# One Hymba block on one core: router and expert weights laid out for contiguous column chunks, and every group's gather made in full precision

## The chip, the cores and the metric

The kernel runs on one core of one Trainium2 chip. The metric is the device time of one execution in microseconds (us); lower is better. The profiler records one execution: its span runs from the first recorded instruction to the last, and the execution's own time is a little longer. Engines are called PE (matrix engine; PEld is its weight loads), DVE (vector), ACT (scalar), POOL and SP (which only issues transfers here).

## What is computed

One encoder block on 512 tokens of width 1024, in float32: two kinds of attention side by side, an output projection, and then a mixture of 32 experts, of which every token uses two. The change touches the mixture only:

```python
h2 = rms_norm(x, g_ffn)                       # x: 512 x 1024, after attention
pg = softmax(h2 @ wg + bg)                    # top 1 of 4 expert groups
le = h2 @ we + be                             # then top 2 of the 8 experts in it
def expert_block(args):                       # xb: the tokens of one expert
    xb, e = args
    return (silu(xb @ w1[e]) * (xb @ w3[e])) @ w2[e]
x = x + combined                              # each token adds its two experts, times its gates
```

w1 and w3 are 1024 x 512 per expert, w2 is 512 x 1024, so an expert has three matrices of 2 MB.

## The kernel before

Attention, projection and router run until about 288 us. From there on 32 experts are worked off in 13 **groups** (`groups`): ten of two experts and three (groups 2, 7 and 12) of four. An expert's weights come as six tiles of 1 MB through a ring of 17 tiles (`slots`, `ring_tile`). SP issues the loads in order (`load_parts`, L715); a load into a ring place waits until PE has read what the place held.

For each group PE goes through these steps, in program order:

- `hidden` (product at L1224): 16 steps. In a step each expert of the group multiplies its own slice of the array's columns (64 columns for two experts, 32 for four), all at once, and a float32 product leaves two records. `hidden` calls what stands in `during[n]` after step n: that is how other work is put between the steps.
- `finish` (L1196) and `turn_hidden` (L1263): small products and transposes that prepare the next two steps.
- `outputs` (L1280): 8 steps of the same kind, with `after[n]` called between them.

Between the steps of a group's `hidden` stand two foreign jobs, both on the array's full width. **Combine** (L1324, L1325) adds the group before into the sum: four blocks of four records, after steps 4, 6, 8 and 10. The **gather** collects the token rows of the next group: a one-hot matrix (`match`, L919, on DVE) times the block's rows `x2`, the result with the model width on partitions, since `hidden` contracts over that. It exists in two forms:

- `gather` / `gather_part` (L928), used for group 0 alone: 32 float32 products of 128 x 128, two records each, the x2 chunk as the weights and the one-hot matrix as the moving operand. The weights of a product are the columns r, r+4, r+8, ... of a half of x2 (every fourth element), because w1, w3 and the router rows were laid out so.
- `quarter` (L1166), used for groups 1 to 12: x2 is split into a rounded half and a remainder (`prepare`: ACT at L1158, DVE at L1159, 192 each in all, two buffers), and the one-hot matrix is the weights. 16 quarters of two records; two quarters are one **lot** of four records. Then the result is copied (`st`, L1172) and transposed back in two `turn`s of four transposes (L1178).

In a group of the steady kind the eight lots of a gather stand so: two in `outputs` of two groups ahead (after steps 4 and 6), six in the following `hidden`, after steps 0, 2, 4, 6, 8 and 10, the last four of them directly behind a combine block. Group 1's gather and that of the group behind `PAUSE` (group 7, whose `hidden` also contains the branch at L1341 for experts with too many tokens) have all eight lots after steps 8 to 15 of `hidden`. Groups 7 and 12 are gathered in hidden 6 and 11. No lots stand in outputs 6 and 11.

Before group 0 there are 48 records of L928, 24 on each side of the router's count (L909, L910, ranked by DVE at L914); 16 more stand in hidden 0 (`first_gather`).

Of the kernel before, what the change touches and what calls it, by code (L numbers as in the profile page):

```python
# [94 lines left out]
def tile_block(ctx: ExitStack, tc: tile.TileContext, a: dict, out: bass.AP):  # L95
# [553 lines left out]
        wv.add(with_split(i, gen))  # L649


    w1 = a["w1"][0].rearrange("e (h p r) f -> e h p (r f)", h=2, p=P)
    w3 = a["w3"][0].rearrange("e (h p r) f -> e h p (r f)", h=2, p=P)
    w2 = a["w2"].rearrange("e c p q j d -> e c p (q j d)")
    NP = NE // 2

# [107 lines left out]
    iota_s = const.tile([P, SLOTS], F32, name="iota_s")  # L764

    def router_loads():
        nc.sync.dma_start(gfp, a["g_ffn"][0].rearrange("(h p r) -> p h r", h=2, p=P))
        raw_r = pool_at.tile([P, KC, 64], F32, tag="qn", name="raw_r", bufs=2)
        parts = {"w_router_g": raw_r[:, 0:1, 0:32], "w_router_e": raw_r[:, 1:5]}
        for n, r in (("w_router_g", 4), ("w_router_e", 32)):  # L770
            parts[n] = parts[n].rearrange("p a b -> p (a b)").rearrange("p (h c) -> p h c", h=2)
            nc.sync.dma_start(parts[n], a[n][0].rearrange("(h p r) c -> p h (r c)", h=2, p=P))
        for src, c0, n in ((a["b_router_g"], 0, 4), (a["b_router_e"], 4, 32)):
            nc.sync.dma_start(rbias[:, c0:c0 + n], bass.AP(tensor=src.tensor, offset=src.offset, ap=[[0, P], [1, n]]))
        nc.gpsimd.iota(desc, pattern=[[-1, 4]], base=4, channel_multiplier=0, allow_small_or_imprecise_dtypes=True)
        nc.gpsimd.iota(iota_s, pattern=[[1, SLOTS]], base=1, channel_multiplier=0,
                       allow_small_or_imprecise_dtypes=True)
        nc.gpsimd.iota(iota_e, pattern=[[1, NE]], base=0, channel_multiplier=0, allow_small_or_imprecise_dtypes=True)
        nc.gpsimd.affine_select(before, ones_f, pattern=[[1, P]], compare_op=ALU.is_gt, fill=0.0,
                                base=0, channel_multiplier=-1)  # L780
        nc.gpsimd.memset(ones_b, 1.0)
        nc.gpsimd.iota(favour, pattern=[[-1, NE]], base=NE - 1, channel_multiplier=0,
                       allow_small_or_imprecise_dtypes=True)
        nc.gpsimd.iota(favour[:, 0:FIXED], pattern=[[-1, FIXED]], base=FIXED, channel_multiplier=0,
                       allow_small_or_imprecise_dtypes=True)
        nc.gpsimd.tensor_scalar(favour[:, 0:FIXED], favour[:, 0:FIXED], 1e6, None, op0=ALU.mult)
        nc.gpsimd.iota(ids, pattern=[[0, 1]], base=0, channel_multiplier=1, allow_small_or_imprecise_dtypes=True)
# [14 lines left out]
    def half_turn(t, h, tag="tr"):  # L802

        xh = x_tile[0][:, t, h * 512:(h + 1) * 512]
        pb = bank(tag)
        xp = xh.rearrange("p (b r) -> p r b", r=4)
        for r in range(4):
            nc.tensor.transpose(pb[:, r * P:(r + 1) * P], xp[:, r], ident)
        x2T[2 * t + h] = pool_raw.tile([P, 4, P], F32, tag="w_raw", name="x2T", bufs=4)
        nc.scalar.copy(x2T[2 * t + h], pb.rearrange("p (k t) -> p k t", k=4))  # L810

# [110 lines left out]
    def gather_part(px, oh, h, ts_):  # L922

        for t in ts_:
            x2 = x_tile[0][:, t, h * 512:(h + 1) * 512].rearrange("p (b r) -> p r b", r=4)
            one = oh[:, t].rearrange("p e s -> p (e s)").bitcast(F32)
            for r in range(4):
                nc.tensor.matmul(px[h][:, r], lhsT=x2[:, r], rhs=one, start=(t == NT - 1 and r == 0),  # L928
                                 stop=(t == 0 and r == 3), skip_group_check=True)
# [206 lines left out]
    def dispatch(oh, p, px=None):  # L1136
# [12 lines left out]
                d["px"] = [bank("sc" if spare else "tr", (P, 4, P)) for _ in range(2)]  # L1149
            gather_part(d["px"], oh, h, ts_)  # L1150

        def prepare(n):

            h, t, q = n // 8, NT - 1 - n // 2 % NT, n % 2
            part = d[n] = wk("part", [P, 2, 256], F32R, bufs=2)
            whole = x_tile[0][:, t, h * 512:(h + 1) * 512].rearrange("p (b r) -> p r b", r=4)[:, 2 * q:2 * q + 2]
            hi, lo = (part[:, m].rearrange("p (r b) -> p r b", r=2) for m in range(2))
            nc.scalar.copy(hi, whole)  # L1158
            nc.vector.tensor_tensor(lo, whole, hi.bitcast(F32), op=ALU.subtract)  # L1159

        def quarter(n, tag="sc"):
            h, t, q = n // 8, NT - 1 - n // 2 % NT, n % 2
            if n % 8 == 0:
                d["rows"] = bank(tag)
            for m in (1, 0):
                nc.tensor.matmul(d["rows"][:, q * 256:q * 256 + 256], lhsT=ohs[t], rhs=d[n][:, m],  # L1166
                                 start=(n % 8 == 0 and m == 1), stop=(n % 8 == 7 and m == 0), skip_group_check=True)
            if n + 2 < 16:
                prepare(n + 2)
            if n % 8 == 7:  # L1170
                d["st"] = wk("st", [P, 512])
                nc.scalar.copy(d["st"], d["rows"])  # L1172

        def turn():
            d["px"] = d["px"] or []
            px = bank("tr", (P, 4, P))
            for r in range(4):
                nc.tensor.transpose(px[:, r], d["st"][:, r * P:(r + 1) * P], ident)  # L1178
            d["px"].append(px)

        def take(h):
            if h == 0:
                xt = None if spare else wk("xt", [P, 2, 4, P])
# [31 lines left out]
            d["oht"], d["gsl"], d["rsl"] = oht, gsl, rsl  # L1215
            yield

        for f in (gather, prepare, quarter, turn, take, finish):
            d[f.__name__] = f
        return d  # L1220

# [62 lines left out]

        return w.rearrange("p (q j d) -> p j q d", j=4, d=256)

    def outputs(t, ht, d, between):

        between, py = iter(between), []
        y = None if isinstance(t["w2", 1, 1], list) else new_y()  # L1290
        for c in range(2):
            py.append(bank("sc"))
            for j in range(4):
                for e, part in enumerate(d["parts"]):
                    w = t["w2", c, e]
                    if isinstance(w, list):
                        for q, wq in enumerate(w):
                            output_product(py[c][:, 256 * q:256 * q + 256], ht, j, part, quarters(wq)[:, j, 0],
                                           q == 0, q == 1)
                    else:  # L1300
                        output_product(py[c].rearrange("p (q d) -> p q d", q=2), ht, j, part, quarters(w)[:, j])
                for f in next(between, ()):
                    f()
            if y:
                put_y(y[0][:, c], y[1][:, c], py[c], d["gsl"])
        return y or put_both(py, d["gsl"])
# [86 lines left out]
    PAUSE = 7  # L1393

    def begin(i):
        d = following[i] = group_dispatch(i)
        d["prepare"](0), d["prepare"](1)

    def call(i, name, *args):
        following[i][name](*args)  # L1400
# [1 line left out]
    for i in range(NG):  # L1402
# [3 lines left out]
        if not last:  # L1406
            rest = ahead if i == 0 else load_parts(i + 1)
            for nxt in islice(rest, 1) if i == PAUSE else rest:
                pass
        during, after = [[] for _ in range(16)], [[] for _ in range(8)]  # L1410
        if i == 0:
            def first_gather(d=d):
                d["gather"](1, (1, 0))
# [3 lines left out]
            during[3] = [turn_places]  # L1417
            during[4] = [first_gather]
            during[7] = [sort_places, partial(begin, 1)]
            during[11] = [lambda d=d: run(d["finish"]("tr"))]  # L1420
        else:
            for n in range(8):
                at_ = (3 if n < 4 else 7) if last else 3 + n // 2 if i == PAUSE else 4 + n // 2 * 2
# [1 line left out]
        if not last:  # L1425
            if i == PAUSE:
                during[7] += [overflow, lambda: list(rest), partial(begin, i + 1)]
                work_on = [(8 + n // 2, "quarter", n) for n in range(16)] + [(13, "turn")]
            elif i + 1 in following and i:
                work_on = [(n // 2 * 2 - 4, "quarter", n) for n in range(4, 16)] + [(6, "turn")]  # L1430
            elif i:
                begin(i + 1)
                work_on = [(n * 12 // 16 + 2, "quarter", n) for n in range(16)] + [(10, "turn")]
            else:
                work_on = [(8 + n // 2, "quarter", n) for n in range(16)] + [(13, "turn")]
            for n, *what in work_on:
                during[n].append(partial(call, i + 1, *what))
        sl = hidden(i, tiles, d, during)
        if not last:
            call(i + 1, "turn")  # L1440
        ht = turn_hidden(sl, iter(()) if last else following[i + 1]["finish"]("o"))
        if last:
            break
        nd = following[i + 1]
        nd["take"](0), nd["take"](1)
        if i + 2 < NG and i + 1 != PAUSE:
            after[0].append(partial(begin, i + 2))
            for n in range(4):
                after[4 + n // 2 * 2].append(partial(call, i + 2, "quarter", n, "mm"))
# [87 lines left out]
```

## Time and profile before

| what | value |
|---|---|
| median of 3 runs | 767.83 us (766.74 to 768.61) |
| the profiled execution's own time | 766.24 us |
| its span | 764.4 us |
| PE busy in the span | 733.8 us (96%) |
| weight loads (PEld) busy | 457.7 us (60%) |
| DVE, ACT, POOL busy | 440.3, 360.0, 91.8 us |
| transfers, mean over the span | 299 GB/s, 228.84 MB |

A mean over the span hides that attention and the experts have different limits, so the experts' stage is read by stretches. In the timeline a row is a run of like instructions: start, length, engine, line, operands, count, and in square brackets an idle time before it with what ended it. Records of PE overlap, so a cost on PE is read from start to start and not by adding up lengths.

### The profile page before, as it was taken

To read this page: it belongs to the slowest core of one execution; us is meant where nothing else is said; L and a number is where in the kernel's file an instruction comes from. 1 tells how busy PE (TensorE), PEld (TensorE's weight loads), DVE (VectorE), ACT (ScalarE), POOL (GpSimd) and SP (SyncE) were. 2 spreads that over 40 slices of the span, in tenths; PEclk is the share of its full clock that TensorE was granted. 3 is DMA by queue.
4 is the path that set the end of the run, shared out by engine and by line. 5 is a ranking of instruction groups with operands and counts; after the bars stand their busy time and mean duration, and the time that the engine had idled before them with its cause. 6 is when DMAs were issued, how large, how long until landed. Compare 5 with 4: busy or idle time off the path is not lost. (4 is left out here: it accounts for less than half of the span.)

```text
span 764.4 us, 13043 instructions
## 1 busy us (share of the span) xinstructions
PE 733.8 (96%) x4748; PEld 457.7 (60%) x4748; DVE 440.3 (58%) x932; ACT 360.0 (47%) x725; POOL 91.8 (12%) x175
## 2 busy tenths in 40 slices
PE   9999999999999999899999999999789999999976
PEld 8899988977889895454444444443234444444223
DVE  4677778776765452565655656563455565565303
ACT  6575867877654421643543434341254344353000
POOL 0302100566663110000000000000000000000000
PEclk9999999999999999999999999999899999999999
DMA  8533111313664955557999999999999999999996
GB/s 312 161 113 91 56 56 55 126 42 111 197 254 172 409 232 208 198 216 316 419 421 420 422 421 419 422 421 419 418 421 421 421 420 420 423 421 420 416 409 258
DMA packets 45902, 228.84 MB, mean 299 GB/s; under 512 B 6885, under 2 KB 9189, under 8 KB 22921
## 3 DMA queue, kind: packets, MB, share of 16 engines
q1 hardware_dynamic: 45688, 227.96, 75.1%
q8 instruction: 38, 0.62, 0.3%
q14 instruction: 32, 0.25, 0.1%
q10 hardware_dynamic: 144, 0.00, 0.0%
HBM read 225.83 MB, written 2.11 MB: 298 GB/s over the span
## 5 line engine op out<-in xcount | busy, mean ns | idle before, releaser
L1158 ACT CAST part<-xs 128x256 fp32r<-128x256 f32 x192 | 119.9, 674 | 121.7 <-PE ps_mm L1166 43.0
L1159 DVE TENSOR_TENSOR part<-xs,part 128x256 fp32r<-128x256 f32 x192 | 115.9, 635 | 58.2 <-ACT part L1158 54.7
L1326 DVE TENSOR_TENSOR sums<-ps_o,sums 128x512 f32<-128x512 f32 x88 | 56.7, 686 | 45.7 <-PE ps_o L1325 45.7
L313 PE MATMUL ps_mm<-w_h,hTl 128*128 128x256 f32 x240 | 69.5, 290 | 0.2
L1224 PE MATMUL ps_mm<-qs,xt 128*64 128x512 f32 (+1 forms) x136 | 68.4, 615 | 1.1 <-DMA qs<-in_w 1.1
L313 PE MATMUL ps_mm<-w_h,hTh 128*128 128x256 f32 x240 | 67.3, 281 | 0.0
L313 PE MATMUL ps_mm<-w_l,hTh 128*128 128x256 f32 x240 | 67.3, 280 | 0.0
L1224 PE MATMUL ps_mm<-mb,xt 128*64 128x512 f32 (+1 forms) x120 | 59.8, 616 | 4.4 <-PEq L1341 4.4
L1224 PE MATMUL ps_mm<-kl,xt 128*64 128x512 f32 (+1 forms) x120 | 60.3, 616 | 0.0
L1224 PE MATMUL ps_mm<-kh,xt 128*64 128x512 f32 (+1 forms) x104 | 50.8, 601 | 0.2 <-DMA kh<-in_w 0.2
L1224 PE MATMUL ps_mm<-w_l,xt 128*64 128x512 f32 (+1 forms) x128 | 50.7, 602 | 0.0
L1224 PE MATMUL ps_mm<-w_h,xt 128*64 128x512 f32 (+1 forms) x120 | 46.8, 601 | 0.0
L313 PEld LDWEIGHTS ps_mm<-w_h,hTl 128*128 128x128 f32 x240 | 45.2, 189 | 1.1 <-DVE hTl L239 0.8
L180 DVE TENSOR_TENSOR w_l<-w_raw,w_h 128x512 fp32r<-128x512 f32 x64 | 44.4, 708 | 1.6 <-ACT w_h L177 1.4
L313 PEld LDWEIGHTS ps_mm<-w_l,hTh 128*128 128x128 f32 x240 | 45.3, 189 | 0.1
L313 PEld LDWEIGHTS ps_mm<-w_h,hTh 128*128 128x128 f32 x240 | 45.2, 188 | 0.0
L518 DVE TENSOR_TENSOR_SCAN p<-p,ones_f 128x513 f32<-128x513 f32 (+3 forms) x32 | 27.5, 859 | 30.6 <-POOL p L513 30.5
L1324 PE MATMUL ps_o<-yl,oht 128*128 128x512 f32 x96 | 43.2, 450 | 0.6 <-DVE sums L1326 0.6
L1253 DVE SCALAR_TENSOR_TENSOR sl<-ps_mm,rsl,sl 128x256 f32<-128x256 f32 x26 | 11.4, 479 | 54.9 <-PE ps_mm L1224 54.9
L1324 PEld LDWEIGHTS ps_o<-yl,oht 128*128 128x128 f32 x96 | 17.9, 187 | 41.8 <-DVE part L1159 24.4
L1267 ACT COPY sl<-ps_mm 128x256 f32<-128x256 f32 x26 | 10.0, 386 | 68.7 <-PE ps_mm L1263 68.7
L177 ACT CAST w_h<-w_raw 128x512 fp32r<-128x512 f32 x64 | 38.2, 621 | 5.2 <-DMA w_raw<-in_w_in 4.9
(299 smaller groups left out, 1781.2 us busy)
## 6 DMA issues: line engine op xcount, KB each, us to landing
qs<-in_w SPq DMA_DIRECT2D x22, 1024.0 KB, 19.8
e<-in_w SPq DMA_DIRECT2D x22, 1024.0 KB, 19.8
kl<-in_w SPq DMA_DIRECT2D x21, 1024.0 KB, 19.8
kh<-in_w SPq DMA_DIRECT2D x21, 1024.0 KB, 19.8
n<-in_w SPq DMA_DIRECT2D x20, 1024.0 KB, 19.8
mb<-in_w SPq DMA_DIRECT2D x20, 1024.0 KB, 19.8
w_h<-in_w SPq DMA_DIRECT2D x20, 1024.0 KB, 19.8
w_l<-in_w SPq DMA_DIRECT2D x20, 1024.0 KB, 19.8
```

What stands on the lines that cost most here:

```text
L177: nc.scalar.copy(part(wh, n), raw[i, n])
L180: eng.tensor_tensor(part(wl, n), raw[i, n], part(wh, n).bitcast(F32), op=ALU.subtract)
L313: nc.tensor.matmul(pb[:, u], lhsT=x(t0 + u, k), rhs=y[:, k], start=first, stop=last, skip_group_check=True)
L518: nc.vector.tensor_tensor_scan(rev, rev, ones_f[:, 0:1].to_broadcast([P, n + 1]), 1.0, op0=ALU.mult, op1=ALU.mult)
L1158: nc.scalar.copy(hi, whole)
L1159: nc.vector.tensor_tensor(lo, whole, hi.bitcast(F32), op=ALU.subtract)
L1224: nc.tensor.matmul(ph[n][part], lhsT=d["xt"][h][:, r, part], rhs=w, start=(h == 0 and r == 0), stop=(h == 1 and r == 3))
L1253: nc.vector.scalar_tensor_tensor(s, ph["w3"][:, c], d["rsl"], s, op0=ALU.mult, op1=ALU.mult)
L1267: nc.scalar.copy(s, pb)
L1324: nc.tensor.matmul(pc, lhsT=oht[:, t], rhs=yl[:, c], start=True, stop=False)
L1326: nc.vector.tensor_tensor(sums[0][:, t, cs], pc, (xs if first else sums[0])[:, t, cs], op=ALU.add)
```

## The change

- On the host, w1, w3, w_router_g, w_router_e and g_ffn get another order of rows, so that a product of `x2` takes 128 neighbouring columns instead of every fourth. The bytes of a load and its rows stay as they were.
- `gather_part` and the transposes for the router (`half_turn`) read neighbouring columns.
- `prepare`, `quarter`, `turn` and the copy `st` are gone. Every group uses `gather`: 32 float32 products in eight lots of four products, that is eight records, after steps 2, 3, 5, 6, 8, 9, 11 and 12 of the `hidden` before (after steps 8 to 15 for group 1 and for the one behind PAUSE). `outputs` has nothing between its steps any more.
- The one-hot matrix of the next group (`begin`) is made at the start of `hidden` instead of in the `outputs` before it. Group 0's `finish` uses another bank of the accumulator memory, "o" for "tr".

The diff, cut to its core:

```diff
-    w1 = a["w1"][0].rearrange("e (h p r) f -> e h p (r f)", h=2, p=P)
-    w3 = a["w3"][0].rearrange("e (h p r) f -> e h p (r f)", h=2, p=P)
+    w1, w3 = (a[n].rearrange("e h p r f -> e h p (r f)") for n in ("w1", "w3"))
...
-        xp = xh.rearrange("p (b r) -> p r b", r=4)
         for r in range(4):
-            nc.tensor.transpose(pb[:, r * P:(r + 1) * P], xp[:, r], ident)
+            nc.tensor.transpose(pb[:, r * P:(r + 1) * P], xh[:, r * P:(r + 1) * P], ident)
...
-            x2 = x_tile[0][:, t, h * 512:(h + 1) * 512].rearrange("p (b r) -> p r b", r=4)
+            x2 = x_tile[0][:, t, h * 512:(h + 1) * 512].rearrange("p (r b) -> p r b", r=4)
             one = oh[:, t].rearrange("p e s -> p (e s)").bitcast(F32)
             for r in range(4):
                 nc.tensor.matmul(px[h][:, r], lhsT=x2[:, r], rhs=one, start=(t == NT - 1 and r == 0),
...
-        def prepare(n):
...
-            nc.scalar.copy(hi, whole)
-            nc.vector.tensor_tensor(lo, whole, hi.bitcast(F32), op=ALU.subtract)
-
-        def quarter(n, tag="sc"):
...
-        def turn():
...
     def begin(i):
-        d = following[i] = group_dispatch(i)
-        d["prepare"](0), d["prepare"](1)
+        following[i] = group_dispatch(i)
...
-            during[11] = [lambda d=d: run(d["finish"]("tr"))]
+            during[11] = [lambda d=d: run(d["finish"]("o"))]
...
-                work_on = [(8 + n // 2, "quarter", n) for n in range(16)] + [(13, "turn")]
-            elif i + 1 in following and i:
-                work_on = [(n // 2 * 2 - 4, "quarter", n) for n in range(4, 16)] + [(6, "turn")]
             elif i:
                 begin(i + 1)
...
+            for n in range(8):
+                at_ = 2 + n * 3 // 2 if i and i != PAUSE else 8 + n
+                during[at_].append(partial(call, i + 1, "gather", n // 4, (NT - 1 - n % 4,)))
         sl = hidden(i, tiles, d, during)
-        if not last:
-            call(i + 1, "turn")
...
-        if i + 2 < NG and i + 1 != PAUSE:
-            after[0].append(partial(begin, i + 2))
-            for n in range(4):
-                after[4 + n // 2 * 2].append(partial(call, i + 2, "quarter", n, "mm"))
-        prev = outputs(tiles, ht, d, after), d["oht"]
+        prev = outputs(tiles, ht, d), d["oht"]
...
+    for n in ("w1", "w3"):
+        data[n] = np.ascontiguousarray(data[n][0].reshape(NE, 2, 4, P, HID).transpose(0, 1, 3, 2, 4))
```

In the lists below x4 counts products, each row is one line of the program on one engine, and the names n, mb, w_h, w_l are ring tiles with weights. PE in `hidden` of group 9, around the first combine block, before:

```order
L1224 MATMUL ps_mm<-n_6557,xt 64x512
L1224 MATMUL ps_mm<-mb,xt 64x512
L1166 MATMUL ps_mm<-part,oh 128x256 x4
L1224 MATMUL ps_mm<-n_6557,xt 64x512
L1224 MATMUL ps_mm<-mb,xt 64x512
L1224 MATMUL ps_mm<-w_h,xt 64x512
L1224 MATMUL ps_mm<-w_l,xt 64x512
L1324 MATMUL ps_o<-yl,oht 128x512
L1325 MATMUL ps_o<-yh,oht 128x512
L1324 MATMUL ps_o<-yl,oht 128x512
L1325 MATMUL ps_o<-yh,oht 128x512
L1166 MATMUL ps_sc<-part,oh 128x256 x4
```

The same place in the changed kernel (L1193 is the product of `hidden`, L1291 and L1292 are combine, L926 is the gather):

```order
L1193 MATMUL ps_mm<-n_6032,xt 64x512
L1193 MATMUL ps_mm<-mb,xt 64x512
L926 MATMUL ps_tr<-oh,xs 128x128 x4
L1193 MATMUL ps_mm<-w_h,xt 64x512
L1193 MATMUL ps_mm<-w_l,xt 64x512
L1291 MATMUL ps_o<-yl,oht 128x512
L1292 MATMUL ps_o<-yh,oht 128x512
L1291 MATMUL ps_o<-yl,oht 128x512
L1292 MATMUL ps_o<-yh,oht 128x512
L1193 MATMUL ps_mm<-w_h,xt 64x512
L1193 MATMUL ps_mm<-w_l,xt 64x512
L926 MATMUL ps_tr<-oh,xs 128x128 x4
```

The lot that stood behind the combine block now stands alone one step later, between two steps of `hidden`.

PE in the second half of `outputs` of group 8, before:

```order
L1280 MATMUL ps_sc<-n_6299,sl_6662 64x512
L1166 MATMUL ps_mm<-part,oh 128x256 x4
L1280 MATMUL ps_sc<-kh,sl_6662 64x512
L1280 MATMUL ps_sc<-n_6299,sl_6662 64x512
L1280 MATMUL ps_sc<-kh,sl_6663 64x512
L1280 MATMUL ps_sc<-n_6299,sl_6663 64x512
L1166 MATMUL ps_mm<-part,oh 128x256 x4
```

and in the changed kernel (L1249 is the product of `outputs`):

```order
L1249 MATMUL ps_sc<-n_5865,sl_6109 64x512
L1249 MATMUL ps_sc<-kh,sl_6109 64x512
L1249 MATMUL ps_sc<-n_5865,sl_6109 64x512
L1249 MATMUL ps_sc<-kh,sl_6110 64x512
L1249 MATMUL ps_sc<-n_5865,sl_6110 64x512
```

Both lots have left `outputs`. DVE from `outputs` of group 8 to the first combine of hidden 9, before (xt: the gathered rows, yl: a rounding remainder of the outputs):

```order
L1186 TENSOR_TENSOR xt<-ps_tr,gfp 128x256 x4
L919 TENSOR_TENSOR oh<-rank_s,iota_s 128x512
L1159 TENSOR_TENSOR part<-xs,part 128x256 x2
L1274 SCALAR_TENSOR_TENSOR yl<-ps_sc,gsl,yh 128x512
L1159 TENSOR_TENSOR part<-xs,part 128x256 x4
L1274 SCALAR_TENSOR_TENSOR yl<-ps_sc,gsl,yh 128x512
L1159 TENSOR_TENSOR part<-xs,part 128x256 x4
L1326 TENSOR_TENSOR sums<-ps_o,sums 128x512 x2
```

and in the changed kernel:

```order
L1183 TENSOR_REDUCE rsl<-g_6592 128x1
L1155 TENSOR_TENSOR xt<-ps_tr,gfp 128x256 x4
L1243 SCALAR_TENSOR_TENSOR yl<-ps_sc,gsl,yh 128x512 x2
L917 TENSOR_TENSOR oh<-rank_s,iota_s 128x512
L1293 TENSOR_TENSOR sums<-ps_o,sums 128x512 x8
```

The one-hot match has moved from ahead of both yl to behind both, and the halves are gone.

## Rows read from the trace of the kernel before

**Rows 1.** Stretches: start:end, length, busy PE PEld DVE ACT POOL, PEclk, DMA share, GB/s.

```profile
333.00:366.00 33.00, 32.99 (x164) 14.97 (x164) 20.47 (x42) 14.78 (x28) 0.00 (x0) 1.00 0.67 267
366.00:530.00 164.00, 163.99 (x892) 73.81 (x888) 96.70 (x186) 68.67 (x125) 0.00 (x0) 1.00 1.01 421
...
710.00:758.00 48.00, 40.43 (x308) 15.61 (x300) 11.20 (x20) 3.92 (x9) 0.00 (x0) 1.00 0.96 383
```

**Rows 2.** Waits of the load queue (SPq), whole span: us in all, times, longest.

```profile
SPq L715 <- PE ps_mm L1224: 64.0, 16, 11.9
```

**Rows 3.** Last group: timeline of PE, and a last line from the chain.

```profile
722.30 0.62 PE L1224 MATMUL ps_mm<-kh,xt 128*32 128x512 f32 x1
...
735.14 1.43 PE L1224 MATMUL ps_mm<-n,xt 128*32 128x512 f32 x3
...
738.71 0.40 PE L1280 MATMUL ps_sc<-mb,sl 128*32 128x256 f32 x1
...
754.99 1.91 PE ps_sc L1280 x26
```

**Rows 4.** Timeline before group 0: router transposes and gather on PE, rank on DVE.

```profile
270.58 1.23 PE L808 MATMUL ps_tr<-ident,xs 128*128 128x128 f32 x8
...
275.35 5.84 PE L928 MATMUL ps_tr<-oh,xs 128*128 128x128 f32 x24 [0.29 <-DVE oh L919]
...
281.49 0.23 DVE L914 SCALAR_TENSOR_TENSOR rank<-ps_o,act 128x64 f32<-128x64 f32 x1 [3.38 <-PE ps_o L1050]
```

**Rows 5.** Timeline, PE in attention: float32 products of 128 x 128, neighbouring columns.

```profile
80.69 0.61 PE L607 MATMUL ps_o<-v,pT 128*128 128x128 f32 x4
...
104.50 1.05 PE L607 MATMUL ps_o<-v,pT 128*128 128x128 f32 x8
```

**Rows 6.** Timeline, PE in hidden 0: first_gather between two steps.

```profile
293.59 4.00 PE L928 MATMUL ps_tr<-oh,xs 128*128 128x128 f32 x16
297.52 0.64 PE L1224 MATMUL ps_mm<-kl,xt 128*64 128x512 f32 x1
```

**Rows 7.** Timeline, PE in hidden 9: a lot alone, a combine with a lot.

```profile
611.94 0.59 PE L1224 MATMUL ps_mm<-n,xt 128*64 128x512 f32 x1
...
612.37 0.59 PE L1224 MATMUL ps_mm<-n,xt 128*64 128x512 f32 x1
...
612.90 0.74 PE L1166 MATMUL ps_mm<-part,oh 128*128 128x256 f32 x4
613.57 0.64 PE L1224 MATMUL ps_mm<-n,xt 128*64 128x512 f32 x1
...
617.44 0.59 PE L1224 MATMUL ps_mm<-w_h,xt 128*64 128x512 f32 x1
...
619.58 0.64 PE L1224 MATMUL ps_mm<-w_h,xt 128*64 128x512 f32 x1
```

**Rows 8.** Timeline, PE in hidden 7: a combine block alone between two steps.

```profile
532.77 0.59 PE L1224 MATMUL ps_mm<-kh,xt 128*32 128x512 f32 x1
...
534.44 0.62 PE L1224 MATMUL ps_mm<-w_h,xt 128*32 128x512 f32 x1
```

**Rows 9.** Waits of PE in 288 to 333 us: us in all, times, longest.

```profile
PE ps_sc L1166 <- DVE part L1159: 3.2, 4, 1.6
PE ps_tr L1178 <- ACT st L1172: 0.7, 1, 0.7
```

**Rows 10.** Timeline, PE in group 7: a lot in hidden, a step of outputs.

```profile
555.12 1.01 PE L1166 MATMUL ps_sc<-part,oh 128*128 128x256 f32 x4
...
570.11 0.59 PE L1280 MATMUL ps_sc<-mb,sl 128*32 128x512 f32 x1
...
573.65 1.04 PE L1280 MATMUL ps_sc<-w_h,sl 128*32 128x512 f32 x2 [1.42 <-DMA w_h<-in_w]
```

**Rows 11.** Timeline, DVE around the start of hidden 9.

```profile
605.87 0.68 DVE L919 TENSOR_TENSOR oh<-rank_s,iota_s 128x512 fp32r<-128x512 f32 x1
...
612.90 0.75 DVE L1274 SCALAR_TENSOR_TENSOR yl<-ps_sc,gsl,yh 128x512 fp32r<-128x512 f32 x1
```

More of the change, by code (lines that the diff above doesn't have):

```diff
@@ L766, in router_loads @@
     def router_loads():
-        nc.sync.dma_start(gfp, a["g_ffn"][0].rearrange("(h p r) -> p h r", h=2, p=P))
+        nc.sync.dma_start(gfp, a["g_ffn"])
         raw_r = pool_at.tile([P, KC, 64], F32, tag="qn", name="raw_r", bufs=2)
@@ L771, in router_loads @@
             parts[n] = parts[n].rearrange("p a b -> p (a b)").rearrange("p (h c) -> p h c", h=2)
-            nc.sync.dma_start(parts[n], a[n][0].rearrange("(h p r) c -> p h (r c)", h=2, p=P))
+            nc.sync.dma_start(parts[n], a[n].rearrange("p h r c -> p h (r c)"))
         for src, c0, n in ((a["b_router_g"], 0, 4), (a["b_router_e"], 4, 32)):
@@ L1150, in gather @@
             gather_part(d["px"], oh, h, ts_)
-        def prepare(n):
[L1154 to L1157, printed above, removed]
-            nc.scalar.copy(hi, whole)
-            nc.vector.tensor_tensor(lo, whole, hi.bitcast(F32), op=ALU.subtract)
-        def quarter(n, tag="sc"):
[L1162 to L1172, printed above, removed]
-        def turn():
[L1175 to L1179, printed above, removed]
         def take(h):
@@ L1216, in finish @@
             yield
-        for f in (gather, prepare, quarter, turn, take, finish):
+        for f in (gather, take, finish):
             d[f.__name__] = f
@@ L1285, in quarters, with outputs @@
         return w.rearrange("p (q j d) -> p j q d", j=4, d=256)
-    def outputs(t, ht, d, between):
-        between, py = iter(between), []
+    def outputs(t, ht, d):
+        py = []
         y = None if isinstance(t["w2", 1, 1], list) else new_y()
@@ L1301, in outputs @@
                         output_product(py[c].rearrange("p (q d) -> p q d", q=2), ht, j, part, quarters(w)[:, j])
-                for f in next(between, ()):
-                    f()
             if y:
@@ L1409, in tile_block @@
                 pass
-        during, after = [[] for _ in range(16)], [[] for _ in range(8)]
+        during = [[] for _ in range(16)]
         if i == 0:
@@ L1427, in tile_block @@
                 during[7] += [overflow, lambda: list(rest), partial(begin, i + 1)]
-                work_on = [(8 + n // 2, "quarter", n) for n in range(16)] + [(13, "turn")]
-            elif i + 1 in following and i:
-                work_on = [(n // 2 * 2 - 4, "quarter", n) for n in range(4, 16)] + [(6, "turn")]
             elif i:
                 begin(i + 1)
[L1433 to L1437, printed above, removed]
+            for n in range(8):
+                at_ = 2 + n * 3 // 2 if i and i != PAUSE else 8 + n
+                during[at_].append(partial(call, i + 1, "gather", n // 4, (NT - 1 - n % 4,)))
         sl = hidden(i, tiles, d, during)
-        if not last:
-            call(i + 1, "turn")
         ht = turn_hidden(sl, iter(()) if last else following[i + 1]["finish"]("o"))
@@ L1526 @@
     data["w_o"] = np.ascontiguousarray(data["w_o"][0].reshape(KC // 2, 2, P, 4, 256).transpose(3, 0, 2, 1, 4))
+    for n in ("w1", "w3"):
+        data[n] = np.ascontiguousarray(data[n][0].reshape(NE, 2, 4, P, HID).transpose(0, 1, 3, 2, 4))
+    for n in ("w_router_g", "w_router_e"):
+        data[n] = np.ascontiguousarray(data[n][0].reshape(2, 4, P, -1).transpose(2, 0, 1, 3))
+    data["g_ffn"] = np.ascontiguousarray(data["g_ffn"][0].reshape(2, 4, P).transpose(2, 0, 1))
     data["w2"] = np.ascontiguousarray(data["w2"][0].reshape(NE, 4, P, 2, 2, 256).transpose(0, 3, 2, 4, 1, 5))
```

## Prediction

> **What bounds the kernel now.** I read the stretches first, then the waits, then the timeline around the places that change. Up to about 366 us the transfers don't run full: 267 GB/s at 67% in 333 to 366 us [rows 1], because SP waits for PE to give ring places back (64.0 us in 16 waits, [rows 2]). From 366 to 530 us both are full: PE is busy for 163.99 of 164 us and the transfers move 421 GB/s [rows 1]. PE never waits there, so every microsecond that is added to PE's row between the steps delays the next group. Only in the last group do the transfers win: in 710 to 758 us PE is busy for 40.43 of 48 us [rows 1]. How much PE waits there is read from starts. A record of `hidden` follows the last after 0.43 us (611.94 to 612.37, [rows 7]), a step is two records, 0.86. In hidden 12 the last record begins 16 records after 722.30 less one, so at 728.75 without waits; it begins at 735.14 + 1.43 - 0.59 = 735.98 [rows 3]. That is 7.2 us. Outputs 12 run from 738.71 to 754.99 + 1.91 = 756.90, 18.2 us [rows 3]; the work in them is 32 half-wide records of 0.215 and two sums as large as a combine block (1.26 below), 9.4 us. That is 8.8 us of waiting. So the last group hides up to 16.0 us of added PE time, and the question is whether the change adds more than this, net of what it saves.
>
> **The price of a lot.** An old lot alone: 612.37 to 613.57 is 1.20, less the 0.43 that a record takes anyway, plus 0.05 since the record behind it is longer (0.64 for 0.59): 0.82 [rows 7]. Combine with a lot is 617.44 to 619.58, likewise 1.76 [rows 7]; combine alone is 532.77 to 534.44, 1.26 to 1.29 [rows 8]. So a lot directly behind a combine costs 0.48, and standing alone 0.35 more: that is the price of going from the experts' column slices to the full array and back. The gather's lot of 16 records in hidden 0 goes from 293.59 to 297.52, 3.93; with the 0.53 ahead of a lot (612.37 to 612.90, [rows 7]), less 0.43 and plus 0.05 as above, it cost 4.08 [rows 6]. From 24 records in 5.84 and 16 in 4.00 a record with every fourth column is 0.23 [rows 4, 6], so again 0.35 to 0.4 is left over.
>
> How fast a record with neighbouring columns goes isn't seen in the gather. The nearest row is attention's product of the same shape and type: 4 records in 0.61, 8 in 1.05, 0.11 a record [rows 5]. The ends are 0.11 and 0.23; I take 0.11, since form, type and column order are those of the new gather. A new lot is 8 x 0.11 + 0.35 = **1.24** alone and 8 x 0.11 + 0.03 = 0.91 behind a combine.
>
> A rule speaks about the 0.35. The rows show it on every lot that stands alone. The Trainium skill, "TensorEngine Tiling (Array Packing)", section Key Properties, says that changing the tiling mode, not just the tile, drains the engine. The trace agrees with 0.35 each time. A steady group goes from 8 such excursions to 10 (four combines and six lots alone, against four and four), so without the drain the sum below would be some 7 us lower, an estimate from 2 x 0.35 in 10 groups.
>
> **The sum, in time order.**
> - Before group 0: 48 records go from 0.23 to 0.11, 5.8 us. DVE idled 3.38 us ahead of the rank [rows 4], so it can take the first half's 2.9 us; I take -5.6. The router's transposes take 8 in 1.23 [rows 4] where 8 products with neighbouring columns take 1.05 [rows 5]; 16 stand there with nothing beside them, -0.4. Together **-6.0**.
> - Hidden 0: `first_gather`, 16 x 0.12 = -1.95. The waits for halves and st go, -3.9 [rows 9], two turns go, -0.5 (four records of 0.11 each; the second lies where PE waits for the end of `hidden` anyway, so I count 0.1 for it). The eight lots are taken like those in hidden 7, which span 1.01 for 0.74 [rows 7, 10] and so cost 1.09, not 0.82: 8 x 0.15 = +1.2. Together **-5.1**.
> - Outputs 0 lose two lots, **-1.6**. Group 1's hidden begins 12.7 us earlier.
> - A steady group: six lots at 1.24 and two at 0.91 come, 9.26; four lots at 0.82, four at 0.48 and the turns' 0.5 go, 5.7. **+3.5** each. Eight groups (1 to 5 and 8 to 10): +28.0. Groups 6 and 11 had only six lots, since their outputs held none: +5.1 each, +10.2.
> - Group 7: eight lots at 1.24 for 1.09, without turns and the wait for st: 0. Its outputs lose two lots, -1.6, and a step whose four experts started 3.5 us apart (570.11 and 573.65, waiting for a weight tile, [rows 10]) has its tile in time, since PE comes later: -3.5. Together **-5.1**.
> - The last group then begins -12.7 + 28.0 + 10.2 - 5.1 = 20.4 us later, and its 16.0 us of waits go. For this the last tile must come before it is needed: seven of its 24 tiles wait for places that its own first steps free; at some 20 us for eight tiles in the queue (8 x 1.05 MB at 421 GB/s, [rows 1]) they land about 754 to 757 us, and the last quarter of the outputs then begins near 760. It fits, barely.
>
> 20.4 - 16.0 = **+4.4 us**. The profiled execution took 766.24 us, 1.6 less than the median of the runs; so 770.6 for it and **772.2** against the median of 767.83.
>
> Costed at nothing: ACT's and DVE's halves (192 each) go, since from 366 us on they lie beside PE's full row [rows 1]. Loads keep their bytes. Where the halves' waits go in hidden 0, nothing is late behind them but PE itself.
>
> **Rivals.** (a) **The transfers stay the bound.** Hidden 1 gets all eight lots, +5.1, and so ends 12.7 - 5.1 = 7.6 us earlier; the ring places that it frees come earlier by this, the full transfers begin and end 7.6 us earlier: 767.8 - 7.6 = 760.2. It decides where PE's sum falls below this, 12 us less over the 80 steady lots, 0.15 a lot: a lot at 1.09 or less. For it: PE's records overlap and are partly modelled, and the weight loads are busy for only 73.81 of 164 us [rows 1]. Against it: the price comes from starts, not from lengths. Between them a lot at 1.18 gives no change (4.4 / 80 = 0.06 less). The Trainium skill, "Perfetto Trace Analysis", section Identifying the Most-Contended Engine, warns that matmul busy share doesn't tell how near PE is to its limit, and to go by weight loads. By that rule PE has room at 45% and this rival would be the likely one; the waits of 0 in 366 to 530 us speak against.
> (b) **The new gather isn't faster than the strided one.** A lot is then 8 x 0.23 + 0.35 = 2.2, about 1 us more, 96 lots: some 85 to 90 us, 860. Against it stand attention's rows [rows 5].
> (c) **A new wait for the one-hot matrix.** DVE ends the second yl at 612.90 + 0.75 = 613.65, 1.71 after hidden 9 began, and the match of 0.68 follows [rows 11], so it is done at 2.4; PE reaches the first lot after three steps, 2.6 [rows 7]. 0.2 us of room. If yl is late by 0.5, PE stands 0.3 to 0.4 in each of 11 groups: 3 to 5 us on top, 775 to 777. Behind the waiting PE stand `hidden` itself and the release of its weights.
>
> **How the numbers follow.** The forecast, lots of 1.20 to 1.3 and PE the bound through the stage, has 0.55; rival (c) 0.10 and (b) 0.03. No change within 0.2% (1.5 us, what a measurement of this kernel can tell) needs lots between 1.16 and 1.20: 0.12. Faster has lots below 1.16 and, at its end, (a): 0.20. So slower 0.68, same 0.12, faster 0.20. The range reaches (a) at 760.2 and (c) with lots of 1.28 (+3 us), 781; it leaves out (b) and the tails. The forecast's own range is 769.4 to 777.
>
> **What would show it.** Eight records of the gather in 1.0 to 1.1 us; a steady group taking 3.5 us longer from hidden to hidden; hidden 0 beginning near 282 us; PE without waits in the last group and the transfers below 421 GB/s before it. It is wrong if a lot alone costs under 1.16, if the last group still waits for weights by several us (then the transfers bind), or if PE waits for the match after step 2.

## The result and the profile after

The changed kernel takes **775.09 us** in the median of 4 runs (773.81 to 776.03) against 767.29 us for the kernel before, a ratio of 1.0099 with a 95% interval of [1.0075, 1.0122]: **about 1% slower**. The forecast was 772.2 us, slower. The profiled execution took 774.29 us with a span of 772.6; before it was 766.24 and 764.4.

Stretches of the changed kernel (columns as in [rows 1]):

```profile
366.00:530.00 164.00, 162.55 (x900) 78.57 (x900) 44.95 (x94) 14.51 (x34) 0.00 (x0) 1.00 1.00 413
...
585.00:732.00 147.00, 145.63 (x740) 69.66 (x740) 41.41 (x90) 13.39 (x33) 0.00 (x0) 1.00 0.95 386
732.00:767.00 35.00, 32.98 (x314) 15.41 (x306) 11.97 (x21) 4.11 (x9) 0.00 (x0) 1.00 0.92 355
```

ACT's busy time in 366 to 530 us fell from 68.67 to 14.51 us and DVE's from 96.70 to 44.95 [rows 1]. None of that shows in the time. PE is as full as it was, and the transfers, which moved 419 GB/s in 585 to 732 us of the kernel before, drop to 386: they now have to wait for PE. The waits of the load queue say it directly (288 to 770 us; us in all, times, longest), against 64.0 us in [rows 2]:

```profile
SPq L714 <- PE ps_mm L1193: 219.6, 45, 14.3
```

What a lot costs, in hidden 9 of the changed kernel, alone and behind a combine block, and the start of hidden 10 (timeline, as [rows 7]):

```profile
621.29 0.59 PE L1193 MATMUL ps_mm<-n,xt 128*64 128x512 f32 x1
...
623.44 0.59 PE L1193 MATMUL ps_mm<-n,xt 128*64 128x512 f32 x1
...
623.97 1.16 PE L926 MATMUL ps_tr<-oh,xs 128*128 128x128 f32 x8
625.06 0.64 PE L1193 MATMUL ps_mm<-n,xt 128*64 128x512 f32 x1
...
627.63 0.59 PE L1193 MATMUL ps_mm<-w_h,xt 128*64 128x512 f32 x1
...
629.29 0.64 PE L1193 MATMUL ps_mm<-w_h,xt 128*64 128x512 f32 x1
...
631.87 0.59 PE L1193 MATMUL ps_mm<-w_h,xt 128*64 128x512 f32 x1
...
633.43 1.05 PE L926 MATMUL ps_tr<-oh,xs 128*128 128x128 f32 x8
634.42 0.64 PE L1193 MATMUL ps_mm<-w_h,xt 128*64 128x512 f32 x1
...
658.09 0.59 PE L1193 MATMUL ps_mm<-e,xt 128*64 128x512 f32 x1
```

Alone: 623.44 to 625.06 is 1.62, less 0.43 and plus 0.05 as in the prediction, **1.24 us**. Combine with a lot: 631.87 to 634.42, likewise 2.17; combine alone, 627.63 to 629.29, takes 1.28 here too, so a lot behind it costs 0.89. From hidden 9 to hidden 10 pass 36.80 us. In the kernel before hidden 9 begins at 611.94 [rows 7] and hidden 10 here, 33.07 later:

```profile
645.01 0.59 PE L1224 MATMUL ps_mm<-e,xt 128*64 128x512 f32 x1
```

The part that saves is at the front. Start of hidden 0 in the kernel before, then start of hidden 0 and `first_gather` in the changed one (`first_gather` before: [rows 6]):

```profile
287.66 0.64 PE L1224 MATMUL ps_mm<-bt,xt 128*64 128x512 f32 x1 [0.52 <-DVE xt L1186]
```

```profile
280.66 0.64 PE L1193 MATMUL ps_mm<-bt,xt 128*64 128x512 f32 x1 [0.52 <-DVE xt L1155]
...
286.06 0.59 PE L1193 MATMUL ps_mm<-kl,xt 128*64 128x512 f32 x1
...
286.59 2.05 PE L926 MATMUL ps_tr<-oh,xs 128*128 128x128 f32 x16
...
288.57 0.64 PE L1193 MATMUL ps_mm<-kl,xt 128*64 128x512 f32 x1
```

Sixteen records that spanned 4.00 us [rows 6] span 2.05. The end, from the chain (start, length, what):

```profile
752.87 10.29 DMA qs<-in_w
...
763.20 1.91 PE ps_sc L1249 x26
```

The last tile lands at 763.16 and PE starts its last row 0.04 later, so at the very end PE still waits for weights a little.

### The profile page after: what moved, and what is told of

It reads as the page before. It is cut to its first block, busy times and chain, and to the rows that moved or that the text cites. A ratio compares the mean times of both kernels' runs of the same rounds, so it can differ in the third digit from the quotient of the medians.

```text
span 772.6 us, 13076 instructions
## 1 busy us (share of the span) xinstructions
PE 750.4 (97%) x5036; PEld 476.9 (62%) x5036; DVE 325.8 (42%) x740; ACT 228.9 (30%) x509; POOL 92.2 (12%) x175
## 5 line engine op out<-in xcount | busy, mean ns | idle before, releaser
L926 PEld LDWEIGHTS ps_tr<-oh,xs 128*128 128x128 f32 x768 | 95.0, 192 | 60.7 <-issue 49.7
L926 PE MATMUL ps_tr<-oh,xs 128*128 128x128 f32 x768 | 108.7, 286 | 1.0 <-DVE oh L917 1.0
L1193 PE MATMUL ps_mm<-qs,xt 128*64 128x512 f32 (+1 forms) x136 | 68.7, 616 | 0.0
L1193 PE MATMUL ps_mm<-mb,xt 128*64 128x512 f32 (+1 forms) x120 | 61.1, 619 | 4.3 <-PEq L1308 4.3
L1193 PE MATMUL ps_mm<-kl,xt 128*64 128x512 f32 (+1 forms) x120 | 60.8, 618 | 0.0
L1217 ACT ACTIVATE sl<-ps_mm,rsl 128x256 f32<-128x256 f32 x26 | 10.9, 471 | 159.2 <-PE ps_mm L1193 143.8
L1193 PE MATMUL ps_mm<-w_l,xt 128*64 128x512 f32 (+1 forms) x128 | 52.7, 606 | 0.0
L1193 PE MATMUL ps_mm<-kh,xt 128*64 128x512 f32 (+1 forms) x104 | 52.0, 607 | 0.0
L1193 PE MATMUL ps_mm<-w_h,xt 128*64 128x512 f32 (+1 forms) x120 | 48.5, 606 | 0.0
L1243 DVE SCALAR_TENSOR_TENSOR yl<-ps_sc,gsl,yh 128x512 fp32r<-128x512 f32 (+1 forms) x28 | 19.9, 712 | 64.3 <-ACT yh L1242 61.7
L1291 PE MATMUL ps_o<-yl,oht 128*128 128x512 f32 x96 | 43.1, 449 | 0.6 <-DVE sums L1293 0.6
L1291 PEld LDWEIGHTS ps_o<-yl,oht 128*128 128x128 f32 x96 | 17.9, 187 | 41.8 <-issue 35.1
## 6 DMA issues: line engine op xcount, KB each, us to landing
mb<-in_w SPq DMA_DIRECT2D x20, 1024.0 KB, 13.2
w_l<-in_w SPq DMA_DIRECT2D x20, 1024.0 KB, 13.3
```

Source lines behind the costliest of these rows:

```text
L1193: nc.tensor.matmul(ph[n][part], lhsT=d["xt"][h][:, r, part], rhs=w, start=(h == 0 and r == 0), stop=(h == 1 and r == 3))
L1217: nc.scalar.activation(s, ph["w1"][:, c], AF.Silu, scale=d["rsl"])
L1243: nc.vector.scalar_tensor_tensor(yl, py, gsl, yh.bitcast(F32), op0=ALU.mult, op1=ALU.subtract)
L1291: nc.tensor.matmul(pc, lhsT=oht[:, t], rhs=yl[:, c], start=True, stop=False)
```

## The experiments

All nine were built from the changed kernel or the kernel before. "Changed" below is 775.09 us; times are medians, ratios are to the kernel before on the same chip.

**What makes a lot dear: its records or its standing alone?** First the lots in pairs behind the combine blocks:

```diff
-                at_ = 2 + n * 3 // 2 if i and i != PAUSE else 8 + n
+                at_ = (4 if i and i != PAUSE else 8) + n // 2 * 2
```

> The changed kernel with its eight lots put in pairs: two lots (16 records) directly behind each of the four combine blocks, and in pairs after steps 8, 10, 12 and 14 for group 1 and the group behind PAUSE. Same products, six fewer separate excursions from the experts' column slices per steady group. Theory (an excursion costs 0.35 us, a record 0.11): a pair behind a combine costs 16 x 0.11 = 1.8, a steady group takes 36.8 - 6 x 0.35 = 34.7 us, the last group begins some 23 us earlier than in the changed kernel (near 708), and then the transfers bind again; they run full earlier than before by the 8 to 12 us that group 1 ends earlier, so about 757 us (754 to 760). Rival 1 (records set the price, wherever they stand): 775. Rival 2 (the transfers can't use the earlier start, they bind where they did before): 766 to 768.

756.66 us (755.14 to 757.54), ratio 0.9872 [0.9842, 0.9901]. The same products in other places are 18 us faster. The timeline of PE in hidden 9:

```profile
610.28 0.59 PE L1193 MATMUL ps_mm<-w_h,xt 128*64 128x512 f32 x1
...
611.84 1.95 PE L926 MATMUL ps_tr<-oh,xs 128*128 128x128 f32 x16
613.72 0.64 PE L1193 MATMUL ps_mm<-w_h,xt 128*64 128x512 f32 x1
```

Combine and pair take 3.44 - 0.43 + 0.05 = 3.06; without combine's 1.28 that is 1.78 for 16 records, 0.11 each and nothing on top. A steady group takes 34.72 us, 2.08 less than changed, as six excursions at 0.35 would have it. Rival 1 is out, and so is rival 2: the end did move, to 10 us below the kernel before on the same chip (766.74).

The opposite, every lot cut in two:

```diff
-                at_ = 2 + n * 3 // 2 if i and i != PAUSE else 8 + n
-                during[at_].append(partial(call, i + 1, "gather", n // 4, (NT - 1 - n % 4,)))
+                for m in range(2):
+                    at_ = min(2 + 2 * n + m, 14) if i and i != PAUSE else 8 + n
+                    during[at_].append(partial(call, i + 1, "gather", n // 4, (NT - 1 - n % 4,), (2 * m, 2 * m + 1)))
```

> The changed kernel with every lot cut in two: 16 half lots of four records after steps 2 to 14 of a steady hidden (four of them together after step 14, four behind a combine). Same products; nine excursions stand alone instead of six. Theory (0.35 an excursion): 1.05 us more in each of ten groups, less up to 2 us that the last group still waits for weights: 783 to 786. Rival (records set the price): 775.

784.49 us (783.61 to 785.17), ratio 1.0234 [1.0207, 1.0261], inside the expected band. A half lot alone:

```profile
629.39 0.59 PE L1193 MATMUL ps_mm<-n,xt 128*64 128x512 f32 x1
...
629.92 0.71 PE L926 MATMUL ps_tr<-oh,xs 128*128 128x128 f32 x4
630.56 0.64 PE L1193 MATMUL ps_mm<-n,xt 128*64 128x512 f32 x1
```

1.17 - 0.43 + 0.05 = 0.79. So alone 4 records cost 0.79, 8 cost 1.24 and `first_gather`'s 16 cost 2.51 - 0.43 + 0.05 = 2.13: 0.35 and 0.11 a record, over a factor of four. That an excursion has a price of its own, which does not grow from 4 to 16 records, is shown. That the price is a drain between tiling modes, as the Trainium skill has it ("TensorEngine Tiling (Array Packing)", Key Properties), fits all of this and isn't separated from another fixed cost at the same boundary.

**Does the layout do it, or the place?** The changed kernel with the old layout:

```diff
-            x2 = x_tile[0][:, t, h * 512:(h + 1) * 512].rearrange("p (r b) -> p r b", r=4)
+            x2 = x_tile[0][:, t, h * 512:(h + 1) * 512].rearrange("p (b r) -> p r b", r=4)
...
+        xp = xh.rearrange("p (b r) -> p r b", r=4)
...
-        data[n] = np.ascontiguousarray(data[n][0].reshape(NE, 2, 4, P, HID).transpose(0, 1, 3, 2, 4))
```

> The changed kernel with the old layout: the same full precision gather at the same places, but a product takes every fourth column of x2. Theory (weight loads of every fourth column set the pitch of a record, 0.23 against 0.11): a lot costs 8 x 0.23 + 0.35 = 2.2, 0.96 more, in 96 lots 92 us; hidden 0 begins 7 us later and first_gather takes 1.95 more: 870 to 878. Rival (the pitch of the strided gather before group 0 belonged to that place, not to the column order): 775 to 785.

871.85 us in one run, as the theory expected. A lot alone, and the weight loads of the gather by their line (ns min/median/max, first and last start) in this kernel and then in the changed one:

```profile
698.52 0.59 PE L1195 MATMUL ps_mm<-n,xt 128*64 128x512 f32 x1
...
699.05 2.14 PE L928 MATMUL ps_tr<-oh,xs 128*128 128x128 f32 x8
701.12 0.64 PE L1195 MATMUL ps_mm<-n,xt 128*64 128x512 f32 x1
```

```profile
L928 PEld LDWEIGHTS ps_tr<-oh,xs x768: 307/329/332, 274.6 to 817.7; 128*128 128x128 f32 x192
```

```profile
L926 PEld LDWEIGHTS ps_tr<-oh,xs x768: 186/192/338, 274.1 to 720.0; 128*128 128x128 f32 x192
```

The lot costs 2.22, a load 329 ns for 192. The gather's products differ in nothing else, so the column order is what makes a record take 0.23 or 0.11. Without the layout the full precision gather is some 104 us slower than the kernel before.

**The saving part alone.** The kernel before with the layout, its halves and transposes kept (the diff is the layout's lines of the change, and in `prepare`):

```diff
-            whole = x_tile[0][:, t, h * 512:(h + 1) * 512].rearrange("p (b r) -> p r b", r=4)[:, 2 * q:2 * q + 2]
+            whole = x_tile[0][:, t, h * 512:(h + 1) * 512].rearrange("p (r b) -> p r b", r=4)[:, 2 * q:2 * q + 2]
```

> The kernel before with the new layout alone: router transposes, group 0's gather and the halves read neighbouring columns, but groups 1 to 12 still gather in halves with transposes, at the old places. Theory: hidden 0 begins 7.0 us earlier and first_gather is 1.95 shorter, as in the changed kernel; steady groups stay at 33.1 us; the transfers run full some 9 us earlier and bind the end, so about 758 us (756 to 761). This is the part of the change that saves. Rival 1: the saving is swallowed by the ring (767). Rival 2: ACT and DVE make the halves faster from neighbouring columns and hidden 0 loses its waits too: 754 to 756.

756.32 us (754.64 to 757.9), ratio 0.9867 [0.9836, 0.9898], within the theory's band and just outside rival 2's; PE's waits for halves in hidden 0 fell only from 3.2 to 2.0 us, so that rival had a small part. The layout saves some 10 us by itself (the kernel before took 766.74 on the same chip). The change as a whole loses 8, so the full precision gather, with its lots where the change places them and the match moved behind both yl, gives back some 18: ten excursions a group instead of eight, and eight records a lot instead of four.

**The end of hidden.** One lot moved to where PE waits:

```diff
-                at_ = 2 + n * 3 // 2 if i and i != PAUSE else 8 + n
+                at_ = (15 if n == 7 else 2 + n * 3 // 2) if i and i != PAUSE else 8 + n
```

> The changed kernel with one lot moved: the last of a steady group's eight stands after step 15 instead of step 12, right ahead of finish, which uses the full array too. Theory (0.35 for the excursion, and the lot covers the time in which PE now waits for the end of the activation, L1232 waiting for sl of DVE, 4.2 us in 11 waits, which a turn covered before): 0.55 us less in each of ten groups, 769.5 to 771 us, and the waits of L1232 gone. Rival 1 (the excursion alone counts, the wait stays): 0.35 less, 771.5. Rival 2 (the last group's transfers, which came within a microsecond of PE, now bind): 773 to 775, with more waits for weights in the last outputs.

764.94 us (764.17 to 766.71, 10 runs), ratio 0.9983 [0.9969, 0.9997]: 10 us below changed, twice what I expected, and a little below the kernel before. The end of hidden 9 in the changed kernel, in this one, and in the kernel before:

```profile
648.93 0.59 PE L1193 MATMUL ps_mm<-mb,xt 128*64 128x512 f32 x1
...
650.30 0.41 PE L1232 MATMUL ps_mm<-ident,sl 128*128 128x128 f32 x2 [0.34 <-DVE sl L1222]
...
651.17 0.64 PE L1249 MATMUL ps_sc<-qs,sl 128*64 128x512 f32 x1
```

```profile
640.63 0.59 PE L1193 MATMUL ps_mm<-mb,xt 128*64 128x512 f32 x1
...
641.16 1.16 PE L926 MATMUL ps_tr<-oh,xs 128*128 128x128 f32 x8
...
643.24 0.64 PE L1249 MATMUL ps_sc<-qs,sl 128*64 128x512 f32 x1
```

```profile
634.35 0.59 PE L1224 MATMUL ps_mm<-mb,xt 128*64 128x512 f32 x1
...
634.88 0.66 PE L1178 MATMUL ps_tr<-ident,st 128*128 128x128 f32 x4
...
636.47 0.64 PE L1280 MATMUL ps_sc<-qs,sl 128*64 128x512 f32 x1
```

From the last step to `outputs` it is 2.24, 2.61 and 2.12 us. Eight records more cost 0.37 instead of 1.24, since PE had stood there for sl: -0.87 a group, 8.7 in ten. I had priced the covered waiting at 0.2, the amount by which a steady group had missed its forecast; the lot covers 0.52 (0.89 less 0.37), of which the profile names 0.34 as a wait for sl. The rest of the 10 us lies elsewhere. Group 7, whose program is the same in both kernels, took 42.57 us for 43.56, at a granted clock of 0.72 and 1.00 in 552 to 558 and 558 to 564 us where the changed kernel's execution had 0.82 and 0.61; that microsecond is not the lot's. Outputs 12 waited 0.4 less. Rivals 1 and 2 are out. The last row also shows what the removed turn had been: four records that made the stretch no longer, as they stood in this wait. Without them it even grew by 0.12; why is not shown.

**What sets the end once PE is out of the way.** All lots in one block, late, early, and late or early in hidden 0 and 7 alone:

```diff
-                at_ = 2 + n * 3 // 2 if i and i != PAUSE else 8 + n
+                at_ = 15
```

> The changed kernel with all eight lots of every gather in one block after step 15 of hidden, right ahead of finish. Theory for PE: no lot stands alone and the block covers the wait for sl; the last run showed 0.37 us net for one lot there, so the block adds 0.37 + 7 x 0.89 = 6.6 us and a steady group takes about 34.2 us (36.8 in the changed kernel, 34.7 with pairs). Theory for the end: with pairs the transfers bind, so only an earlier start of the full transfers helps; the steps of hidden 0 and 1 now run up to 7 us earlier, since no gather stands between them, and give ring places back earlier: 749 to 754 us. Rival 1 (the start of the full transfers hangs on when group 1 ends, not on its steps): 755 to 756, as with pairs. Rival 2 (with the gather done late, the next hidden waits for DVE's xt): over 757, with a new wait of L1193 for xt.

**750.90 us** (750.46 to 753.01, 5 runs), ratio 0.9794 [0.9771, 0.9817]: 16 us below the kernel before, 24 below the changed one, and the best of all kernels here. It lies in the theory's band, below that of rival 1 and far from rival 2's. A steady group takes 34.19 us.

```diff
-                at_ = 2 + n * 3 // 2 if i and i != PAUSE else 8 + n
+                at_ = 4 if i and i != PAUSE else 8
```

> The same block of eight lots, but early: directly behind the first combine block (after step 4; after step 8 for group 1 and the one behind PAUSE). PE's sum per steady group is that of the pairs (8 x 0.89, 34.7 us), but steps 5 to 15 come up to 5 us later than with pairs, and with them the ring places. Theory (the time at which hidden 0 and 1 give ring places back sets the start of the full transfers, and these bind the end): 757 to 760. Rival (only PE's sum counts): 756.5, as with pairs.

754.60 us (754.15 to 755.28), ratio 0.9839 [0.9815, 0.9863]: 2 us below the pairs, with overlapping intervals of the ratios, where I had expected 1 to 3 above; the rival's 756.5 was missed as well. I had overlooked that one block in hidden 0 stands alone once where the pairs stand alone four times: hidden 0 takes 30.24 us here and 31.26 with the pairs, 1.0 less, as three excursions would have it. The next two were to separate the two places:

```diff
-                at_ = 2 + n * 3 // 2 if i and i != PAUSE else 8 + n
+                at_ = 4 + n // 2 * 2 if i and i != PAUSE else 8
```

> Pairs behind the combine blocks in the steady groups, as with the pairs before, but hidden 0 (and the group behind PAUSE) gets its eight lots in one block after step 8. It differs from the early block only in the steady groups, and from the pairs only in hidden 0 and 7. Theory A (three fewer excursions in hidden 0 bring groups 1 and on forward by 1.7 us, and where the lots stand in hidden 1 makes no difference): as the early block, 754.6 us. Theory B (the early block in hidden 1 did cost time, and hidden 0 gained more than that): 752 to 753.5.

756.02 us (754.57 to 756.81), ratio 0.9838 [0.9815, 0.986]. As a time it is in neither band. As a ratio it is the early block's, 0.9839, as theory A has it: the kernel before took 768.21 us on this chip and 767.31 on that of the early block. The profiled execution gives another reason for the longer time: hidden 0, the same program in both kernels, ran at a lower clock here. Two stretches of 6 us of this kernel, and then of the early block (columns as in [rows 1], the last three are PEclk, DMA share and GB/s):

```profile
294.00:300.00 6.00, 5.42 (x35) 4.92 (x31) 1.03 (x3) 0.00 (x0) 0.00 (x0) 0.72 0.70 295
300.00:306.00 6.00, 6.00 (x46) 4.54 (x46) 0.00 (x0) 0.00 (x0) 0.00 (x0) 1.00 0.00 0
```

```profile
294.00:300.00 6.00, 5.42 (x49) 5.33 (x48) 0.62 (x2) 0.00 (x0) 0.00 (x0) 1.00 0.65 270
300.00:306.00 6.00, 6.00 (x39) 3.51 (x39) 0.21 (x2) 0.70 (x3) 0.00 (x0) 1.00 0.08 11
```

At a mean of 0.72 the block of 64 records spans 8.88 us, at 1.00 it spans 7.41 (timeline, below): 1.5 us, about the difference between 756.0 and 754.6. Either reason alone would make it theory A; both together would come closer to B, and the second rests on the clock of one execution. So whether it matters where the lots stand in hidden 1 is not settled to better than a microsecond.

```profile
295.08 8.88 PE L926 MATMUL ps_tr<-oht,xs 128*128 128x128 f32 x64 [0.58 <-DVE oht L917]
```

```profile
294.67 7.41 PE L926 MATMUL ps_tr<-oht,xs 128*128 128x128 f32 x64 [0.58 <-DVE oht L917]
```

```diff
-                at_ = 2 + n * 3 // 2 if i and i != PAUSE else 8 + n
+                at_ = 4 + n // 2 * 2 if i and i != PAUSE else 15
```

> The same, with the block of hidden 0 (and of the group behind PAUSE) after step 15; pairs in the steady groups. Theory (what is moved by 360 us sets the end; hidden 0's steps give their ring places back up to 7 us earlier): 752 to 753.5, about half of the way from 754.6 to the 750.9 of the kernel with all blocks at the end, whose other half comes from hidden 1. Rival (hidden 0 alone counts): 751.

753.52 us (752.66 to 755.32), ratio 0.9817 [0.9793, 0.984], at the upper edge of the theory's band, and the rival's 751 lies below all five runs: hidden 0 alone doesn't make up the gain of the block at the end.

The stretches just shown hold the mechanism: while the block stands in the middle of hidden 0, the transfers stop, 0 and 11 GB/s in 300 to 306 us, since no step gives a ring place back: from 290 to 312 us the load queue waits for products of `hidden` for 19.5 and 18.1 us, three times each, at most 10.6 and 9.1 at once. With the block at the end, where these waits sum to 10.0 us, they don't stop:

```profile
300.00:306.00 6.00, 6.00 (x50) 5.10 (x47) 0.88 (x2) 0.13 (x1) 0.00 (x0) 1.00 0.95 369
```

How much had been moved by 360 us then tells the end. The stretch 282 to 360 us of the kernel before, with the layout alone, pairs, the early block and the block at the end:

```profile
282.00:360.00 78.00, 73.47 (x365) 39.12 (x366) 37.77 (x99) 31.02 (x58) 1.80 (x5) 1.00 0.56 216
```

```profile
282.00:360.00 78.00, 75.24 (x398) 35.79 (x392) 33.85 (x97) 26.00 (x67) 0.00 (x0) 0.98 0.69 269
```

```profile
282.00:360.00 78.00, 76.74 (x454) 40.68 (x451) 20.08 (x61) 10.04 (x22) 0.00 (x0) 1.00 0.70 272
```

```profile
282.00:360.00 78.00, 76.72 (x465) 41.80 (x464) 20.38 (x56) 10.04 (x22) 0.00 (x0) 1.00 0.71 278
```

```profile
282.00:360.00 78.00, 77.99 (x476) 40.79 (x476) 21.59 (x58) 10.04 (x22) 0.00 (x0) 1.00 0.75 296
```

| kernel | GB/s in 282 to 360 | ahead of before, at 421 GB/s | last tile lands (chain) | ahead of before |
|---|---|---|---|---|
| before | 216 | | 754.95 | |
| layout alone | 269 | 9.8 us | 745.07 | 9.9 us |
| pairs | 272 | 10.4 us | 744.76 | 10.2 us |
| early in hidden 0 and 7 | 270 | 10.0 us | 744.96 | 10.0 us |
| early block | 278 | 11.5 us | 743.36 | 11.6 us |
| late in hidden 0 and 7 | 287 | 13.2 us | 741.62 | 13.3 us |
| block at the end | 296 | 14.8 us | 739.88 | 15.1 us |

The third column is (GB/s less 216) x 78 us / 421. It gives the fifth within 0.3 us in every kernel. This is bookkeeping as long as the transfers run full from 360 us on, and they do in these kernels, at 420 to 421 GB/s from 360 to 700 us. So it is not PE that sets the end there but how much has been moved before. The changed kernel moved 263 GB/s by 360 and could have landed 8.7 us before the kernel before; it landed 8.2 after, because it couldn't keep the transfers full (386, above). That is PE as the bound, shown from the other side.

## Why the prediction was right, and where its sum was off

The direction and the cause held: PE is the bound, with lots at 1.24 and 0.91 forecast and 1.24 and 0.89 measured. The size held less well: +8.2 us from profile to profile and +7.8 between the medians, for +4.4. Luck had a part in its being this near: the front saved a microsecond more than forecast, which offset some of two misses the other way, 2.6 us in the steady groups and 2.0 in outputs 12. The moves, from starts in the two timelines:

| place | forecast | measured |
|---|---|---|
| start of hidden 0 | -6.0 | 287.66 to 280.66, -7.0 |
| hidden 0 | -5.1 | -4.9 |
| outputs 0 | -1.6 | -1.7 |
| eight steady groups | +28.0 | +19.4 (1 to 5), +11.2 (8 to 10), 30.6 |
| groups 6 and 11 | +10.2 | +10.7 |
| group 7 | -5.1 | -5.5 |
| hidden 12 | -7.2 | -7.2 |
| outputs 12 | -8.8 | -6.8 |
| sum | +4.4 | +8.2 |

- **Before hidden 0** it is 1.0 us better than forecast. The gather's two halves fell by 2.9 each, as counted, and the 16 transposes by 0.2 for 0.4. A lead of 0.98 us is there already ahead of them, when the router's products begin (267.61 us for 268.59); what gave it isn't separated.
- **A steady group** takes 3.7 us more, not 3.5. The term that failed is the turn at the end of hidden: I counted 0.1 for its removal, as a saving. It had stood in the wait for sl, and its removal cost 0.12 (2.12 to 2.24). PE's named waits (288 to 770 us) show it in the first row below; the kernel before has that wait once, 0.7 us, in the last group:

```profile
PE ps_mm L1232 <- DVE sl L1222: 4.2, 11, 0.8
PE ps_tr L926 <- DVE oh L917: 0.7, 1, 0.7
...
PE ps_tr L926 <- DVE oht L917: 0.6, 1, 0.6
```

- **Rival (c)**, the wait for the one-hot matrix, came in hidden 0 (0.6) and hidden 1 (0.7) and nowhere else: the 0.2 us of room that the rows gave was enough in the other groups. It makes hidden 1 0.8 us dearer than the other steady groups. (The upper end of the range, 781, adds up to 780 from the terms given, 777 and 3.)
- **The last group** keeps 1.7 to 2 us of waiting for weights. I had its last tile land at 754 to 757 us, in time; it lands at 763.16. The term was mis-sized: I reckoned with eight tiles still to come, 20 us of transfers, once the first steps of hidden 12 had freed places. But from the start of hidden 12 to the landing there are 31.40 us at 378 GB/s, which is 11.3 tiles of 1.05 MB (row below, columns as in [rows 1]). The load queue's last wait for PE that the profile names, for `outputs` of group 11, ends about when hidden 12 begins; from 738 us on it issues half a tile every 1.3 us, waiting only for earlier loads. So the transfers had fallen behind before the last group, while PE was the bound, and the last group itself began 1.8 us later than forecast.

```profile
731.80:763.20 31.40, 29.38 (x275) 12.71 (x273) 10.63 (x18) 3.70 (x8) 0.00 (x0) 1.00 0.98 378
```

- **Rival (a)**, the transfers as the bound, needed lots at 1.09 or less. With the pairs a lot costs 0.89, and there the transfers bind: 756.7 us, with 760.2 forecast for that case. Its page's rule, that the weight loads' share (beside the share of peak arithmetic) tells PE's room and the busy share doesn't (the Trainium skill, "Perfetto Trace Analysis", Identifying the Most-Contended Engine), would have had the changed kernel go that way. It didn't: PE bound it with weight loads busy for 78.57 of 164 us.
- **Rival (b)** fell: 0.11 a record.

## What to carry to other kernels

Where packed products in column slices fill PE, every visit to the full array has a fixed price besides its records, here 0.35 us; put foreign work directly behind other foreign work, or where PE waits anyway, before its precision or form is changed. Take work out from under a wait only after asking what it had covered. When transfers bind the end, what counts is how early the ring's places come back, so foreign work belongs behind the steps that free them and not between these.

## What the runs showed of the hardware that I had not expected

- A float32 record of 128 x 128 holds its pace of 0.11 us although its weight load is recorded as 192 ns; with every fourth column the load is 329 ns and the pace 0.23. The load's length is not the pace, but its growth shows up in it.
- The granted clock fell to 0.72 in 294 to 300 us of one execution and stayed at 1.00 in another of the same program up to that place, both after the same idle of 0.58 us (PE waiting for the one-hot matrix). In 296 to 298 us the row says 0.50, the lower of the two levels, 1.2 and 2.4 GHz. It cost 1.5 us. The layout alone's execution has 0.72 in the same stretch, after an idle of 0.92 us. In group 7 the clock also fell, in the kernel before and in the changed one, while PE waited 4.4 and 4.3 us, and stayed low for some microseconds behind the wait (0.56 in 546 to 552 us, 0.61 in 558 to 564). So differences of a microsecond between single executions show nothing.
